# The second row of each q and k block starts later, and the copy of its transposes is queued two half chunks behind them

## The chip, the cores and the metric

The kernel runs on one core of one Trainium2 chip. The metric is the device time of one launch in microseconds (us). The core has a matrix engine (PE, with its weight loads PEld), a vector engine (DVE), a scalar engine (ACT), a general engine (POOL) and an engine that issues most transfers (SP). Each works through its own queue in the order in which the program issued its instructions, and waits on the others by semaphores.

## The reference

One layer of a hybrid block for 256 positions of width 2048, in float32:

```python
xn = rms_norm(x, norm1_g)
q, k, v, ga, gg = split(xn @ w_in)              # q, k: 4 heads x 2 x 128; v: 4 heads x 256
q = apply_rope(rms_norm(q, q_norm_g), cos, sin)
k = apply_rope(rms_norm(k, k_norm_g), cos, sin)
att = rms_norm(diff_attention(q, k, v, lam), subln_g) * (1 - lambda_init)
u = silu(layer_norm(causal_depthwise_conv(ga * sigmoid(gg), conv_w, conv_b)))
h = x + concat([att, u]) @ w_out
y = h + (silu(rms_norm(h) @ w_gate) * (rms_norm(h) @ w_up)) @ w_down
```

`diff_attention` makes two softmax maps for each head and subtracts lam times the second from the first. The mask lets a query see the 64-wide chunks up to its own.

## The kernel before

**Chunks.** All weights stream through the core in chunks. In the first part of the kernel a chunk is 256 rows of one 512-column block (two k-tiles of 128 rows). Each chunk n is loaded (SP, line 315), rounded to a high part by ACT (line 320, here called whi(n)), and the rest is taken by DVE (line 329, here wlo(n)). PE then multiplies in two halves: half A is eight matmuls with the high weights (lines 359 and 360), half B is four matmuls with the low weights (line 365). There are three buffers each for high and low parts, so whi(n) can run only when half A of chunk n-3 is through. Rounding and splitting are issued two chunks ahead (`run_chunks`, lines 387 to 419).

**Chunk numbers.** The blocks follow one another: chunks 0 to 32 are the convolution's columns, 33 to 40 k block 0, 41 to 48 q block 0, 49 to 56 k block 1, 57 to 64 q block 1, 65 to 72 v block 0, 73 to 80 v block 1. Then comes w_out: 81 and 82, 83 and 84, 85 and 86 are its first three column blocks with rows 0 to 511 (attention heads 0 and 1), 87 to 92 the same column blocks with rows 512 to 1023 (heads 2 and 3, head 3 first in chunk 88), 93 to 104 the convolution's rows, 105 to 112 the last column block. Gate, up and down projections follow until the end.

**Steps between the chunks.** All other work is written as generators. `resume()` (line 244) is called after each half chunk and advances every running generator to its next `yield`; `lag(n)` (line 250) lets n half chunks pass. What a generator issues lands in the engines' queues at that place. Convolution taps (DVE, line 517) are put in by `run_side` as long as a credit lasts (1.30 us more per half chunk; each wlo, tap and listed step spends some).

**The q and k rows.** When a block is summed, `qk_done` (line 590) starts one `qk_rows` generator (line 606) per 128 positions (m = 0 and 1, the two rows). A row issues: 4 squares on ACT (lines 612 and 427), three small operations on POOL for the scale fq (lines 217, 218, 615); 3 half chunks later 4 scaled copies qn on ACT (line 619); 2 later the rotation on DVE (lines 626 to 629); 6 later, as soon as an auxiliary bank is free (`room`, line 257: of the 4 auxiliary PSUM banks `held[0]` are counted as taken), 4 transposes on PE (line 634) and, right behind them, the copy to qT or kT on ACT (line 635), after which the row counts as placed. The second row starts two half chunks behind the first.

**Who waits for the rows.** After a q block `qk_done` waits until all four rows of q and k are placed, and starts `attend_scores` for two heads, 4 half chunks apart (lines 595 to 602). A head's steps, each some half chunks after the one before: scores on PE (line 649), maximum on DVE (657, 659), exponentials on ACT (668), reciprocal on DVE (677) and a small product a on POOL (679), p on ACT (688), the difference wt on DVE (695), 3 transposes on PE (701 to 703) and their copy on ACT (706). `v_done` (709) copies v out of its sum banks on ACT (712) and starts `attend_values` (718): once the head's 706 is issued, products with v on PE (727), squares (427) on ACT, their scale ro on POOL (217, 218), att on ACT (738), 4 transposes on PE (746) and the split into high part (233, ACT) and low part (234, DVE) for w_out.

**Sum banks.** There are 4 for the chunks, two per block in turn, so that chunk 83 takes the two of v block 1.

**Where w_out waits for a head.** `operand()` (line 332) asks for the split attention output; if the step that makes it has not been issued, it issues all taps that are left and calls `resume()` until it is there, with no matmuls between.

Of the kernel before, what the change touches and what calls it, by code (L numbers as in the profile page):

```python
# [64 lines left out]
AUX = 4  # L65

LAG = (3, 2, 6)
HL_BUFS = 3

KTILE_US = 1.30  # L70
# [52 lines left out]
def tile_block(  # L123
# [82 lines left out]
    def negative_lambda():  # L206

        le = const.tile([P, 2], F32, tag="le", name="le")
        act.activation(le, ls, AF.Exp)
        pool.tensor_tensor(neg_lam, le[:, 1:2], le[:, 0:1], ALU.subtract)  # L210
        pool.tensor_scalar(neg_lam, neg_lam, 1.0, -LAMBDA_INIT, ALU.mult, ALU.add)

    def rsqrt_mean(dst, ss, n, eps):

        k = dst.shape[-1]
        t = small.tile([P, 8], F32, tag="rsq", name="rsq")
        pool.tensor_scalar(t[:, :k], ss, 1.0 / n, eps, ALU.mult, ALU.add)
        pool.tensor_tensor(dst, t[:, :k], neghalf[:, :k], ALU.pow)
# [22 lines left out]
    def start(gen):  # L241
        running.append(gen)
# [7 lines left out]
    def lag(n):  # L250
        for _ in range(n):
            yield


    held = [0]

    def room(n, hold=0):
        while held[0] + n > AUX:
            yield
        held[0] += hold  # L260
# [6 lines left out]
    def spend(us):  # L267
        credit[0] -= us
# [49 lines left out]
    def round_chunk(c):  # L318
        c["hi"] = c["view"](wp.tile([P, NK * N], F32R, tag="whi", name="whi", bufs=HL_BUFS))
        act.copy(c["hi"], c["raw"])  # L320
        if c["by_dma"]:
            c["lo"] = c["view"](wp.tile([P, NK * N], F32R, tag="wlo", name="wlo", bufs=HL_BUFS))
            act.activation(c["lo"], c["raw"], AF.Copy, scale=-1.0)
            pool.dma_start(out=c["lo"], in_=c["raw"].bitcast(F32R), accum_op=ALU.add)

    def split_chunk(c):
        if not c["by_dma"]:
            c["lo"] = c["view"](wp.tile([P, NK * N], F32R, tag="wlo", name="wlo", bufs=HL_BUFS))
            dve.tensor_tensor(c["lo"], c["raw"], c["hi"].bitcast(F32), ALU.subtract)  # L329
# [95 lines left out]
    def square_sum(src, accum, **kw):  # L425
        junk = pre.tile([P, N], F32, tag="junk", name="junk", bufs=1)
        act.activation(junk[:, : src.shape[-1]], src, AF.Square, accum_out=accum, **kw)
# [162 lines left out]
    def qk_done(key, b, ps):  # L590
        for m in range(NM):
            yield
            start(qk_rows(key, b, m, ps[m]))
            yield
        if key == "q":
            while not all((k, b, m) in placed for k in "qk" for m in range(NM)):
                yield
            if b == 0:
                negative_lambda()
            for hd in (2 * b, 2 * b + 1):  # L600
                start(attend_scores(hd))
                yield from lag(4)
# [3 lines left out]
    def qk_rows(key, b, m, ps):  # L606

        G = N // DH
        spend(1.65)
        ss = small.tile([P, G], F32, tag="ssq", name="ssq")  # L610
        for j in range(G):
            square_sum(ps[:, j * DH : (j + 1) * DH], ss[:, j : j + 1], scale=rstd1[m])
        f = small.tile([P, G], F32, tag="fq", name="fq")
        rsqrt_mean(f, ss, DH, EPS)
        pool.tensor_scalar(f, f, rstd1[m], 0.0, ALU.mult, ALU.add)
        yield from lag(LAG[0])
        qn = pre.tile([P, G, DH], F32, tag="va", name="qn")
        for j in range(G):
            act.activation(qn[:, j, :], ps[:, j * DH : (j + 1) * DH], AF.Copy, scale=f[:, j : j + 1])
        yield from lag(LAG[1])  # L620
        t1 = pre.tile([P, G, DH], F32, tag="vb", name="t1")
        t2 = pre.tile([P, G, DH], F32, tag="vc", name="t2")
        tab = gcs[key, m]
        hd = DH // 2
        bc = lambda ap, n: ap.unsqueeze(1).to_broadcast([P, G, n])
        dve.tensor_tensor(t1, qn, bc(tab[:, 0, :], DH), ALU.mult)
        dve.tensor_tensor(t2[:, :, :hd], qn[:, :, hd:], bc(tab[:, 1, :hd], hd), ALU.mult)
        dve.tensor_tensor(t2[:, :, hd:], qn[:, :, :hd], bc(tab[:, 1, hd:], hd), ALU.mult)
        dve.tensor_tensor(t1, t1, t2, ALU.add)
        yield from lag(LAG[2])  # L630
        yield from room(1)
        pt = aux_ps.tile([P, G, P], F32, tag="aux", name="ps_qk")
        for j in range(G):
            pe.transpose(pt[:, j, :], t1[:, j, :], ident)
        act.copy(qkT[key][:, b * G : (b + 1) * G, m * P : (m + 1) * P], pt)
        placed.add((key, b, m))

# [536 lines left out]
    for b in range(2):  # L1174
        done += [lambda ps, key=key, b=b: qk_done(key, b, ps) for key in "kq"]
# [71 lines left out]
```

## Time and profile before

| | |
|---|---|
| median of 3 runs | 1048.78 us (1048.51 to 1048.9) |
| the profiled execution's own time | 1048.92 us |
| its span | 1047.1 us |
| PE busy | 1036.2 us, 99% of the span |
| DVE, ACT, POOL busy | 900.6, 621.6, 100.5 us |
| granted PE clock | 1.00 in every stretch |

The span is what the profile covers; 1.8 us of the execution's own time lie around it. In the rows of a timeline stand the start in us from the span's start, the duration in us, the engine, the line, the operation with output and inputs, and in brackets how long the engine was idle before it and who released it. Matmuls overlap, so the start of one to the start of the next is what a matmul costs, not its duration. Chunk n's half B (line 365, x4) is the mark by which a chunk can be found: chunk 54 has it at 157.86 us, chunk 56 at 164.74, chunk 72 at 215.39, chunk 77 at 235.84, chunk 82 at 249.94, chunk 88 at 272.65.

### The profile page before, as it was taken

The page shows a single profiled execution, that of the slowest core. Times are in us where ns is not written, and L with a number is a line of the kernel's source. Part 1 is how long each engine was busy: PE and PEld are TensorE (multiplying, and loading weights), DVE is VectorE, ACT ScalarE, POOL GpSimd, SP SyncE. Part 2 cuts the span into 40 slices and gives each one's busy share as a digit, 9 for nine tenths or more (in the row PEclk, how much of TensorE's full clock was granted, in tenths as well). Part 3 has the DMA queues.
Part 4 walks back from the last instruction along what each step waited for, and adds up shares of the span by engine and source line. Part 5 has one row for each costly group of instructions (what it writes and reads, how often), then busy time and mean ns, then how long its engine had stood idle before and what let it go on. Part 6 is the DMA issues. An engine that isn't in the chain of part 4 may idle for free.

```text
span 1047.1 us, 12933 instructions
## 1 busy us (share of the span) xinstructions
PE 1036.2 (99%) x4663; PEld 852.5 (81%) x4663; DVE 900.6 (86%) x1095; ACT 621.6 (59%) x786; POOL 100.5 (10%) x143
## 2 busy tenths in 40 slices
PE   9999999999999999999999999999999999999998
PEld 7888887877788788888888888888888888888886
DVE  7899889898765599999787898999878789989897
ACT  7544666755756565776463657666644446657442
POOL 0130122201100100000001010000000110000010
PEclk9999999999999999999999999999999999999999
DMA  9657654453546566987867789879757879798683
GB/s 335 227 182 280 212 163 167 154 181 134 177 153 226 194 223 214 268 266 236 232 210 188 217 271 273 256 217 285 248 175 241 219 208 291 222 287 267 187 265 85
DMA packets 113936, 231.30 MB, mean 221 GB/s; under 512 B 7504, under 2 KB 8656, under 8 KB 113616
## 3 DMA queue, kind: packets, MB, share of 16 engines
q1 hardware_dynamic: 104864, 203.71, 56.9%
q0 software_dynamic: 8864, 26.74, 13.4%
q8 instruction: 36, 0.59, 0.2%
q14 instruction: 28, 0.23, 0.1%
q10 hardware_dynamic: 144, 0.03, 0.0%
HBM read 204.24 MB, written 9.44 MB: 204 GB/s over the span
## 4 chain that ended last, share of the span: by engine, by line
PE 61%; DMA 2%; DVE 2%; issue 1%; ACT 0%; DVEq 0%; POOLq 0%
PE q L1020 12%; PE q L1014 12%; PE q L1015 12%; PE q L995 8%; PE q L993 7%; PE q L994 7%; DMA raw<-in_w_down_dram 1%; PE ps_a L831 1%; DMA wlo<-raw 1%; PE acc L365 1%; PE acc L359 1%; PE acc L360 1%; DVE wlo L329 1%; DVE wlt L976 0%; DVE wt L966 0%
## 5 line engine op out<-in xcount | busy, mean ns | idle before, releaser
L320 ACT CAST whi<-raw 128x1024 fp32r<-128x1024 f32 (+1 forms) x273 | 281.5, 1048 | 141.6 <-PE acc L360 58.9
L329 DVE TENSOR_TENSOR wlo<-raw,whi 128x1024 fp32r<-128x1024 f32 (+1 forms) x239 | 287.8, 1218 | 73.5 <-ACT whi L320 73.3
L972 ACT CAST wh<-wt 128x2048 fp32r<-128x2048 f32 x52 | 99.6, 1914 | 77.6 <-DVE wt L968 76.9
L976 DVE TENSOR_TENSOR wlt<-wt,wh 128x2048 fp32r<-128x2048 f32 x52 | 119.1, 2290 | 14.9 <-ACT wh L972 14.7
L359 PE MATMUL acc<-whi,xhi 128*128 128x512 f32 x320 | 126.9, 397 | 1.0 <-ACT whi L320 0.9
L360 PE MATMUL acc<-whi,xlo 128*128 128x512 f32 x320 | 125.2, 391 | 0.0
L1014 PE MATMUL q<-whi,chi 128*128 128x512 f32 x320 | 125.2, 391 | 0.0
L1015 PE MATMUL q<-whi,clo 128*128 128x512 f32 x320 | 124.5, 389 | 0.0
L993 PE MATMUL q<-wh,fhi 128*128 128x512 f32 x280 | 109.9, 393 | 0.0
L994 PE MATMUL q<-wh,flo 128*128 128x512 f32 x280 | 109.1, 390 | 0.0
L517 DVE SCALAR_TENSOR_TENSOR y<-upad,cw,y 128x256 f32<-128x256 f32 x240 | 102.2, 482 | 2.2 <-ACT y L510 2.2
L1014 PE MATMUL q<-whi,ahi 128*128 128x512 f32 x256 | 100.2, 391 | 0.0
L1015 PE MATMUL q<-whi,alo 128*128 128x512 f32 x256 | 99.6, 389 | 0.0
L975 DVE TENSOR_TENSOR wlb<-wb,wh 128x1536 fp32r<-128x1536 f32 x52 | 91.1, 1752 | 1.8 <-ACT wh L969 1.8
L365 PE MATMUL acc<-wlo,xhi 128*128 128x512 f32 x320 | 87.8, 396 | 2.0 <-DVE wlo L329 2.0
L1020 PE MATMUL q<-wlo,chi 128*128 128x512 f32 x320 | 85.7, 390 | 0.2 <-DMA wlo<-raw 0.2
L969 ACT CAST wh<-wb 128x1536 fp32r<-128x1536 f32 x52 | 76.6, 1474 | 0.0
L365 PEld LDWEIGHTS acc<-wlo,xhi 128*128 128x128 f32 x320 | 59.7, 189 | 15.3 <-DVE wlo L329 3.3
L359 PEld LDWEIGHTS acc<-whi,xhi 128*128 128x128 f32 x320 | 60.4, 189 | 14.3 <-ACT whi L320 1.9
L1020 PEld LDWEIGHTS q<-wlo,chi 128*128 128x128 f32 x320 | 59.9, 188 | 13.2 <-DMA wlo<-raw 0.8
L360 PEld LDWEIGHTS acc<-whi,xlo 128*128 128x128 f32 x320 | 60.4, 189 | 12.2
L1014 PEld LDWEIGHTS q<-whi,chi 128*128 128x128 f32 x320 | 60.1, 188 | 12.3
(230 smaller groups left out, 1739.1 us busy)
## 6 DMA issues: line engine op xcount, KB each, us to landing
raw<-in_w_in_dram SPq DMA_DIRECT2D x79, 512.0 KB, 4.6
raw<-in_w_down_dram SPq DMA_DIRECT2D x64, 512.0 KB, 7.2
raw<-in_w_gate_dram SPq DMA_DIRECT2D x48, 512.0 KB, 7.5
raw<-in_w_up_dram SPq DMA_DIRECT2D x48, 512.0 KB, 6.2
wb<-in_w_up_dram SPq DMA_DIRECT2D x40, 512.0 KB, 3.7
wb<-in_w_gate_dram SPq DMA_DIRECT2D x40, 512.0 KB, 4.9
wlo<-raw POOLq DMA_DIRECT2D x34, 512.0 KB, 7.1
raw<-in_w_out_dram SPq DMA_DIRECT2D x32, 512.0 KB, 4.2
```

What stands on the lines that cost most here:

```text
L320: act.copy(c["hi"], c["raw"])
L329: dve.tensor_tensor(c["lo"], c["raw"], c["hi"].bitcast(F32), ALU.subtract)
L359: pe.matmul(ps[m], xhi[:, ms], hi[:, j, :], start=c["first"] and j == 0, stop=False)
L360: pe.matmul(ps[m], xlo[:, ms], hi[:, j, :], start=False, stop=False)
L365: pe.matmul(ps[m], xhi[:, ms], lo[:, j, :], start=False, stop=c["last"] and j == nk - 1)
L517: dve.scalar_tensor_tensor(y[:, ct, :], src, wk, y[:, ct, :], ALU.mult, ALU.add)
L976: dve.tensor_tensor(lot, c["t"], c["hi"][:, :SUMMED].bitcast(F32), ALU.subtract)
L993: pe.matmul(ps, hi, c["hi"][:, w], start=bool(first), stop=False)
L994: pe.matmul(ps, lo, c["hi"][:, w], start=False, stop=False)
L1014: pe.matmul(ps, xs[i][0][:, ms], hi[:, i, :], start=i == 0 and bool(c["first"].get(qs[m])), stop=False)
L1015: pe.matmul(ps, xs[i][1][:, ms], hi[:, i, :], start=False, stop=False)
L1020: pe.matmul(sum_bank(c, qs[m]), xs[i][0][:, ms], lo[:, i, :], start=False, stop=i == 1 and bool(c["last"].get(qs[m])))
```

## The change

`qk_done` lets four half chunks pass, where it was one, between the start of a row and the next turn of its loop, so the second row starts five half chunks behind the first instead of two. In `qk_rows` the auxiliary bank of the transposes is counted as held until the copy is issued, and the copy (and with it the mark that the row is placed) is issued two half chunks behind the transposes. Nothing is computed differently, and no instruction is added or taken away.

```diff
+ROWS_APART, COPY_LAG = 4, 2
@@ qk_done
         for m in range(NM):
             yield
             start(qk_rows(key, b, m, ps[m]))
-            yield
+            yield from lag(ROWS_APART)
@@ qk_rows
         yield from lag(LAG[2])
-        yield from room(1)
+        yield from room(1, 1)
         pt = aux_ps.tile([P, G, P], F32, tag="aux", name="ps_qk")
         for j in range(G):
             pe.transpose(pt[:, j, :], t1[:, j, :], ident)
+        yield from lag(COPY_LAG)
+        held[0] -= 1
         act.copy(qkT[key][:, b * G : (b + 1) * G, m * P : (m + 1) * P], pt)
         placed.add((key, b, m))
```

## The prediction

> **What bounds the kernel now.** I read the page's busy times first, then who PE waited for in the stretch that the change touches (120 to 300 us), then the stretches, then the timelines of PE, DVE, ACT and POOL there.
>
> ```profile
> PE 1036.2 (99%) x4663; PEld 852.5 (81%) x4663; DVE 900.6 (86%) x1095; ACT 621.6 (59%) x786; POOL 100.5 (10%) x143
> PE acc L365 <- DVE wlo L329: 2.0, 2, 1.2
> PE acc L359 <- DVE mchi L582: 0.6, 1, 0.6
> PE ps_o L727 <- ACT qT L706: 0.6, 1, 0.6
> PE ps_o L727 <- ACT v L712: 0.3, 1, 0.3
> 60.00:120.00 60.00, 60.00 (x273) 49.66 (x272) 59.62 (x109) 29.02 (x35) 1.53 (x3) 1.00 0.66 231
> ```
>
> PE is the bound: 99% busy, so a microsecond in which PE stands still is a microsecond of the kernel, and what other engines gain is worth nothing by itself. In the touched stretch PE stood still for 2.0 + 0.6 + 0.6 + 0.3 = 3.5 us. That is the ceiling of any gain. DVE is full in the convolution part (59.62 of 60 us), so it has little room to catch up. PE's issue order loses or gains no instruction.
>
> ```profile
> 148.50 3.40 POOL L218 TENSOR_TENSOR fq<-rsq,neghalf 128x4 f32<-128x4 f32 x1
> 152.31 1.14 ACT L619 ACTIVATE qn<-acc,fq 128x128 f32<-128x128 f32 x4 [1.61 <-POOL fq L615]
> 154.42 1.23 DVE L329 TENSOR_TENSOR wlo<-raw,whi 128x1024 fp32r<-128x1024 f32 x1 [3.39 <-ACT whi L320]
> 155.56 0.68 DVE L626 TENSOR_TENSOR t<-qn,gcsq 128x512 f32<-128x512 f32 x1
> 157.56 1.27 DVE L517 SCALAR_TENSOR_TENSOR y<-upad,cw,y 128x256 f32<-128x256 f32 x3
> 158.75 1.22 DVE L329 TENSOR_TENSOR wlo<-raw,whi 128x1024 fp32r<-128x1024 f32 x1
> 159.89 0.68 DVE L626 TENSOR_TENSOR t<-qn,gcsq 128x512 f32<-128x512 f32 x1
> 155.14 1.07 PE L365 MATMUL acc<-wlo,xhi 128*128 128x512 f32 x4
> 157.86 1.07 PE L365 MATMUL acc<-wlo,xhi 128*128 128x512 f32 x4
> 164.74 1.20 PE L365 MATMUL acc<-wlo,xhi 128*128 128x512 f32 x4 [0.80 <-DVE wlo L329]
> 215.39 1.20 PE L365 MATMUL acc<-wlo,xhi 128*128 128x512 f32 x4 [1.24 <-DVE wlo L329]
> ```
>
> This shows how the two larger waits come about. A chunk is 2.72 us of PE (157.86 - 155.14). A row's rotation is 2.0 us of DVE (155.56 to 157.56), a tap 0.4, a wlo 1.14 (158.75 to 159.89). ACT stood for fq, whi(54) came late, DVE stood 3.39 us, and then got two rotations in two successive chunks: 2.0 + 3 x 0.4 + 1.14 = 4.3 us for chunk 55, with a fourth tap 4.7 for chunk 56. Against 2.72 it falls back 1.6 and then 2.0 us; its lead at chunk 54 was 157.86 - 155.65 = 2.2. So PE waited 0.80 at chunk 56, and 1.24 by the same pattern at chunk 72.
>
> **The change part by part.** Nothing is added; steps move.
>
> *The rotations five half chunks apart.* In the new order the DVE work before each wlo, from chunk 55, is: one rotation, 3 taps, 3 taps, rotation with 4 taps. With wlo that is 3.1, 2.3, 2.3, 4.7 us, or +0.4, -0.4, -0.4, +2.0 against PE. The furthest DVE falls back is 1.6, inside its lead of 2.2: the wait of 0.80 goes. The same holds for 1.24 at chunk 72. The wait of 0.3 for v goes too, since its product moves two chunks on. **Gain 2.0 + 0.3 = 2.3.** The bounds are 0 (waits stay) and 2.3.
>
> *The copy two half chunks later.* Its bank is held meanwhile. Counted through the code, no step is refused a bank for it. With the second row 3 half chunks later, the block's last copy is 5 later, so all four heads start 5 half chunks later. The blocks that do not depend on them (v, w_out) stay. The rest of the sum is what is late then.
>
> *Chunks 68 to 74.* ACT's new queue there is: p, four exponentials, whi(68), squares, whi(69), copy, p, qn, whi(70), copy, squares, whi(71). By the rows below an exponential group is 1.6 us, p 0.8, a whi 0.95; the squares are about as long as the exponentials, qn 1.0. That makes about 13 us in the time of four chunks, 10.9 plus about 1.2 of inserted PE work. ACT falls back about 1 us from a lead of up to 2, and fq can cost it as much again. **Loss between 0 and 1.7; I take 0.5**, nearer to the load, which rows show, than to the waits.
>
> ```profile
> 235.84 1.18 PE L365 MATMUL acc<-wlo,xhi 128*128 128x512 f32 x4
> 241.48 0.36 ACT L668 ACTIVATE pr<-ps_s,nmx 128x128 f32<-128x128 f32 x1
> 243.08 1.05 ACT L320 CAST whi<-raw 128x1024 fp32r<-128x1024 f32 x1
> 239.61 0.17 DVE L657 MEMSET ps_s<- 64x128 f32 x1
> 241.06 1.27 DVE L517 SCALAR_TENSOR_TENSOR y<-upad,cw,y 128x256 f32<-128x256 f32 x3
> 248.69 0.22 DVE L677 RECIPROCAL r<-sm 128x2 f32<-128x2 f32 x2
> 249.38 0.90 ACT L688 ACTIVATE p<-pr,a 128x128 f32<-128x128 f32 x2 [3.99 <-POOL a L679]
> 250.19 0.46 ACT L706 COPY qT<-ps_wt 128x384 f32<-128x384 f32 x1
> 246.85 1.07 PE L365 MATMUL acc<-wlo,mahi 128*128 128x512 f32 x4
> 249.94 1.07 PE L365 MATMUL acc<-wlo,mahi 128*128 128x512 f32 x4
> 254.54 1.08 PE L365 MATMUL acc<-wlo,mahi 128*128 128x512 f32 x4
> 193.27 1.95 POOL L679 TENSOR_TENSOR a<-r,neg_lam 128x1 f32<-128x1 f32 x2 [6.87 <-DVE r L677]
> ```
>
> *Chunk 83 waits for v.* Count from E, the half B of chunk 77 (235.84), behind head 1's transposes: DVE needs these, so its lead is set anew there. In before, head 3's reciprocal stands 12.85 later; ACT waits 0.69 for a, p takes 0.81. Now head 2's reciprocal stands at this place, behind 1.4 us more DVE work (a maximum of 1.45 for a wt of 0.66, two taps, less a reciprocal). Behind its p ACT has head 3's exponentials (1.60, 241.48 to 243.08) and only then v, whose first half takes 0.64. That is 12.85 + 1.4 + 0.69 + 0.81 + 1.60 + 0.64 = E + 18.0, and 0.3 to 0.9 more by how much later DVE reaches E. Chunk 83 takes the banks of v block 1, so its first matmul waits for this copy. It began at 254.54 - 8 x 0.227 = E + 16.9 in before. Now the 0.37 of a head's transposes at chunk 81 (3.09 against 2.72) and the 1.88 of the product at chunk 82 (4.60 against 2.72) come later, and head 3's scores (1.36) come before: E + 16.0. **Loss 2.0 to 2.9; I take 2.4.**
>
> *Chunk 84 waits for head 2's copy.* Then ACT has whi(84), whi(85), head 3's p, whi(86), and behind them this copy (706), for which PE stands behind half A of chunk 84. DVE: wlo(84) at E + 21.2, wt, reciprocal at 22.0; a between 0.7 and 1.95; p, whi(86), copy: E + 24.9 to 26.2. PE would start the product at E + 24.0 (18.4 + 2.72 + 1.81 + the 1.06 from transposes to product that the pattern takes in before). **Loss 1.0 to 2.3; I take 1.6.** Both ends of these two losses reach down to 0 if DVE should be a chunk further ahead.
>
> ```profile
> 257.27 0.27 PE L701 MATMUL ps_wt<-ident,wt 128*128 128x128 f32 x1
> 258.33 1.56 PE L727 MATMUL ps_o<-v,qT 128*128 128x256 f32 x6 [0.57 <-ACT qT L706]
> 261.29 0.47 ACT L233 ACTIVATE ahi<-ps_at,cols 128x256 fp32r<-128x256 f32 x1 [2.27 <-PE ps_at L746]
> 261.80 0.48 DVE L234 SCALAR_TENSOR_TENSOR alo<-ps_at,cols,ahi 128x256 fp32r<-128x256 f32 x1 [2.09 <-ACT ahi L233]
> 262.32 0.47 ACT L233 ACTIVATE ahi<-ps_at,cols 128x256 fp32r<-128x256 f32 x1 [0.55 <-DVE alo L234]
> 262.69 0.38 ACT L427 ACTIVATE junk<-ps_o 128x256 f32<-128x256 f32 x1
> 263.56 1.04 ACT L320 CAST whi<-raw 128x1024 fp32r<-128x1024 f32 x1
> 265.08 0.84 ACT L738 ACTIVATE att<-ps_o,ro 128x256 f32<-128x256 f32 x2 [0.48 <-POOL ro L218]
> 255.20 1.95 POOL L218 TENSOR_TENSOR ro<-rsq,neghalf 128x2 f32<-128x2 f32 x1
> ```
>
> *Chunk 88 waits for head 3.* Its split was issued 3 half chunks before chunk 88 and comes 4 later. So `operand` issues it by one resume ahead of chunk 88's first matmul, with nothing between. Count from X, the end of half A of chunk 86. PE: transposes of head 3 (0.33), of head 2 (0.44), product (start X + 1.0, 1.2), half B and chunk 87: X + 5.9; unhindered, chunk 88's second matmul would start at about X + 6.5. ACT: copy, the two halves of head 2's split 1.03 apart, squares (0.87) done at X + 3.3; ro 1.5 to 2.6; att 0.74; whi(90) 0.95; the first high part 0.5. DVE: wlo(90), then the low part: X + 8.2 to 9.3, which that matmul needs. **Loss 1.7 to 2.8; I take 2.2.** With ACT and DVE free it would still be about 1.0, the high and low part one behind the other.
>
> **Sum:** -2.3 + 0.5 + 2.4 + 1.6 + 2.2 = +4.4 on the profiled execution's 1048.92, which lies 0.14 above the median: 1053.3, or **1053.2** against the median.
>
> [...]
>
> **The rivals.**
> - *Nothing is gained.* The squares that covered fq's 3.40 us now come behind qn, so ACT may wait as long and DVE stand its 3.39 still; if both waits stay, 1055.2. Against it: the rotations are no longer in successive chunks.
> - *Not slower.* DVE's lead at chunk 77 decides. If head 2's reciprocal comes 3 us earlier from E than I reckon, v and the copy are in time, and chunk 88 costs 1.5: -2.3 + 1.5, 1048.0. For it: DVE's 3.39 of idle time may be filled. Against it: E is set by PE, and 12.85 of the 14.25 us is DVE work of before.
> - *The clock.* A wait of PE longer than any here (the largest is 1.24) might bring down the granted clock, 1.00 so far; a chunk at half the clock is 2.72 more, 1055.9 or above. [...]
> - *Faster* would take chunk 88 at 0 as well, which nothing shows.
>
> **How the numbers follow.** Forecast 0.60 (by its own bounds 1051 to 1056.5), nothing gained 0.12, clock 0.06, not slower 0.17, faster 0.05. Range 1049.8 to 1057: it leaves out most of the last two and little above. A measurement of this kernel tells about 0.2% (2.1 us) from no change: slower 0.78, same 0.17, faster 0.05.
>
> **What would show it.** In the changed profile: no PE wait for wlo at chunks 56 and 72; a wait of line 359 for v (712) of 2 us or more at chunk 83; a longer wait of line 727 for line 706 at chunk 84; a wait of lines 359 and 360 for the split (233, 234) of head 3 at chunk 88. If DVE's reciprocal of head 2 lies less than 12 us behind E, the two middle terms are wrong; if lines 359 and 360 don't wait at chunk 88, the fourth is.

## The result, and the profile after

The changed kernel takes **1051.78 us** (median of 14 runs, 1051.25 to 1057.92) against 1048.77 for the kernel before beside it (14 runs, 1048.0 to 1050.59): 1.0031 times as long, 95% interval 1.0023 to 1.0039. The profiled execution took 1051.79 us (span 1050.0), 2.87 more than the profiled one of before. Lines 68 and on of before are one higher in the new kernel, those from 635 on three higher.

The page's busy times, and PE's waits between 120 and 300 us (who waits, for whom; us in total, times, longest):

```profile
PE 1036.6 (99%) x4663; PEld 853.5 (81%) x4663; DVE 901.1 (86%) x1095; ACT 624.1 (59%) x786; POOL 101.7 (10%) x143
```
```profile
PE acc L360 <- ACT v L715: 2.1, 1, 2.1
PE acc L361 <- DVE alo L235: 0.8, 1, 0.8
PE acc L360 <- DVE mchi L583: 0.6, 1, 0.6
PE acc L360 <- ACT ahi L234: 0.6, 1, 0.6
PE ps_o L730 <- ACT qT L709: 0.6, 1, 0.6
```

Busy times tell little: PE's is 0.4 us longer. The waits tell more. The two for wlo are gone, as is the 0.3 for v at a product. In their place stand 2.1 us for v, and 0.6 and 0.8 for a split (lines 234 and 235). Idle time went from 3.5 to 4.7 us, 1.2 of the 2.9 that the kernel is slower; PE's timeline and the granted clock (the column ahead of the DMA share) show more:

```profile
246.94 1.07 PE L366 MATMUL acc<-wlo,mahi 128*128 128x512 f32 x4
250.14 0.50 PE L360 MATMUL acc<-whi,mahi 128*128 128x512 f32 x1 [2.13 <-ACT v L715]
...
251.21 0.63 PE L361 MATMUL acc<-whi,malo 128*128 128x512 f32 x1
...
253.34 1.52 PE L366 MATMUL acc<-wlo,mahi 128*128 128x512 f32 x4
254.70 0.39 PE L360 MATMUL acc<-whi,mahi 128*128 128x512 f32 x1
257.58 1.56 PE L730 MATMUL ps_o<-v,qT 128*128 128x256 f32 x6 [0.57 <-ACT qT L709]
271.84 0.50 PE L360 MATMUL acc<-whi,ahi 128*128 128x512 f32 x1 [0.62 <-ACT ahi L234]
273.12 0.50 PE L361 MATMUL acc<-whi,alo 128*128 128x512 f32 x1 [0.78 <-DVE alo L235]
```
```profile
250.00:251.00 1.00, 0.86 (x3) 0.58 (x4) 0.02 (x1) 1.00 (x3) 0.00 (x0) 0.93 0.82 252
251.00:252.00 1.00, 1.00 (x3) 0.78 (x3) 0.37 (x1) 1.00 (x2) 0.00 (x0) 0.50 0.96 272
252.00:253.00 1.00, 1.00 (x4) 0.74 (x3) 1.00 (x2) 0.55 (x1) 0.00 (x0) 0.50 1.04 403
253.00:254.00 1.00, 1.00 (x4) 0.81 (x3) 1.00 (x6) 0.00 (x0) 0.33 (x1) 0.50 0.37 127
254.00:255.00 1.00, 1.00 (x5) 0.77 (x5) 1.00 (x3) 0.41 (x1) 1.00 (x2) 0.86 0.83 256
```

Behind the wait of 2.13 us a matmul lasts 0.63 us instead of 0.39 (start to start 0.43 instead of 0.227), until about 254: the granted clock was 0.50. That is loss too, and no view of waits or busy time has it (PE counts as busy). From the column: 0.07 + 3 x 0.50 + 0.14 = 1.71 us.

To place gain and loss, take the start of each chunk's half B in both traces and subtract. The differences against before, set to 0 at chunk 55 (the profiled executions start up to 0.4 us apart; by chunk 98 nothing changes any more), for this kernel and some of those below. The chunk columns come from one execution of each kernel, the profiled one, whose own time stands beside the median; in filled and v_early it was the slowest:

| kernel | median us | profiled us | chunk 81 | 83 | 84 | 87 | 88 | 98 |
|---|---|---|---|---|---|---|---|---|
| after | 1051.78 | 1051.79 | -2.99 | -1.56 | -1.11 | +0.21 | +2.73 | +2.76 |
| filled | 1052.33 | 1054.73 | -2.99 | -2.71 | -1.20 | +1.69 | +5.47 | +5.89 |
| v_early | 1054.29 | 1055.18 | -2.99 | -5.24 | -1.18 | +1.91 | +5.58 | +6.09 |
| v_early_filled | 1049.99 | 1050.61 | -2.99 | -5.24 | -2.33 | -1.05 | +1.49 | +1.51 |
| head3_early | 1052.5 | 1052.23 | -2.99 | -1.83 | -1.10 | +1.36 | +1.62 | +3.73 |
| p_late | 1047.69 | 1047.26 | -2.99 | -5.24 | -5.21 | -3.76 | -1.28 | -1.28 |
| p_late3 | 1050.19 | 1050.3 | -2.99 | -5.24 | -5.21 | -2.63 | -2.37 | +1.32 |

(In chunks 82 to 87 lie attention products and transposes whose place moved, so that the columns 83 to 87 compare only kernels with the same places.) The change gains 3.0 us up to chunk 81 and loses 5.7 from 82 to 88.

How the two waits of chunks 83 and 84 come about stands in ACT's timeline, with POOL's and DVE's:

```profile
246.30 0.23 DVE L680 RECIPROCAL r<-sm 128x2 f32<-128x2 f32 x2
246.99 0.91 ACT L691 ACTIVATE p<-pr,a 128x128 f32<-128x128 f32 x2 [4.24 <-POOL a L682]
249.39 1.28 ACT L715 ACTIVATE v<-acc,rstd 128x512 f32<-128x512 f32 x2
250.53 2.01 ACT L321 CAST whi<-raw 128x1024 fp32r<-128x1024 f32 x2
254.12 0.41 ACT L691 ACTIVATE p<-pr,a 128x128 f32<-128x128 f32 x1 [1.57 <-POOL a L682]
255.65 0.51 ACT L691 ACTIVATE p<-pr,a 128x256 f32<-128x256 f32 x1 [1.13 <-POOL a L682]
256.07 1.04 ACT L321 CAST whi<-raw 128x1024 fp32r<-128x1024 f32 x1
257.05 0.48 ACT L709 COPY qT<-ps_wt 128x384 f32<-128x384 f32 x1
```

First head 2's p and four exponentials of head 3 (247.8 to 249.4) stand ahead of v, then head 3's p stands ahead of the copy out of head 2's transposes, and itself waits 1.57 and 1.13 us for a.

### The profile page after: what moved, and what is told of

It is laid out like the page before. It is cut to its first block, busy times and chain, and to the rows that moved or that the text cites. A ratio compares the mean times of both kernels' runs of the same rounds, so it can differ in the third digit from the quotient of the medians.

```text
span 1050.0 us, 12935 instructions
## 1 busy us (share of the span) xinstructions
PE 1036.6 (99%) x4663; PEld 853.5 (81%) x4663; DVE 901.1 (86%) x1095; ACT 624.1 (59%) x786; POOL 101.7 (10%) x143
## 4 chain that ended last, share of the span: by engine, by line
PE 62%; DVE 1%; DMA 1%; issue 0%; ACT 0%; DVEq 0%
PE q L1017 12%; PE q L1023 12%; PE q L1018 12%; PE q L998 8%; PE q L996 8%; PE q L997 8%; PE acc L366 1%; DMA wlo<-raw 1%; PE ps_a L834 1%; PE acc L360 1%; PE acc L361 1%; DVE wlo L330 0%; DVE wlt L979 0%; DVE wt L969 0%; ACT wh L975 0%
## 5 line engine op out<-in xcount | busy, mean ns | idle before, releaser
L321 ACT CAST whi<-raw 128x1024 fp32r<-128x1024 f32 (+1 forms) x273 | 282.0, 1049 | 153.9 <-PE acc L361 67.7
L1018 PEld LDWEIGHTS q<-whi,clo 128*128 128x128 f32 x320 | 60.1, 188 | 12.3
```

Of the source, the lines that this page charges most:

```text
L1018: pe.matmul(ps, xs[i][1][:, ms], hi[:, i, :], start=False, stop=False)
```

## The experiments

My theory after this: gain and loss are two things. The rows' distance takes the waits for wlo away; what comes back is a queue on ACT, in which what PE needs next (v, then head 2's copy) stands behind steps that nobody needs yet, and the half clock behind the long wait adds to it (1.71 us behind 2.13). The rival: the gain is PE's lead over ACT and DVE, which comes back at the heads whatever their order.

**filled.** PE is kept busy in the wait for v.

```diff
+        if c is chunks[83]:
+            warm_up(18)        # transposes of the identity into a bank of their own
```

> The changed kernel with 18 transposes of the identity (into a spare bank, results unused) put on PE between chunk 82 and chunk 83, where PE stood 2.13 us for v and then ran at half the clock for about 3 us. Theory (the clock's loss takes the place of the wait for head 2's copy at chunk 84): no gap at chunk 83, clock 1.00 all through, but PE now waits some 1.8 us more than 0.57 for that copy behind half A of chunk 84, and the time stays within 0.6 of the changed kernel's 1051.8. Rival (the clock's loss of 1.7 us comes on top of everything): no new wait at chunk 84, 1050.1.

1052.33 us (1.0031, 1.0020 to 1.0043). PE's waits, and the granted clock:

```profile
PE ps_o L732 <- ACT qT L711: 2.1, 1, 2.1
```
```profile
259.00:262.00 3.00, 3.00 (x9) 2.32 (x8) 1.99 (x4) 2.58 (x7) 0.89 (x2) 0.50 0.76 255
276.00:279.00 3.00, 3.00 (x12) 2.59 (x11) 0.00 (x0) 0.72 (x2) 0.00 (x0) 0.50 0.58 220
```

The clock stays up at chunk 83 (1.00 up to 258 us), but PE comes to chunk 84 earlier, waits 2.1 us there for head 2's copy, and the half clock follows that wait. As theory had it, the second wait stood behind the first; what it had not is another stretch of half clock, behind the 0.64 and 0.78 us of chunk 88. That is the profiled execution, the slowest of six (1054.73; the fastest took 1051.04).

**v_early.** v's second block is copied (line 715) right behind chunk 80, ahead of head 3's exponentials, where `v_done` runs one half chunk later.

```diff
-    def v_done(b, ps):
-        yield
+    def v_copy(b, ps):
         for m in range(NM):
             act.activation(v_sb[m][:, b * N : (b + 1) * N], ps[m], AF.Copy, scale=rstd1[m])
+    def v_start(b, ps):        # called when the block is summed
+        if b:
+            v_copy(b, ps)
+        return v_done(b, ps)
+    def v_done(b, ps):
+        yield
+        if not b:
+            v_copy(b, ps)
```

> The changed kernel with the copies of v block 1 issued right behind chunk 80, ahead of head 2's p and head 3's exponentials in ACT's queue. Theory (chunk 83 stands for v because ACT does head 3's exponentials first): the wait at chunk 83 and the half clock go (4.1 us), and the wait for head 2's copy behind half A of chunk 84 grows by 1.9 to 3.3 since PE is there earlier; about 1050.4, between 1049.7 and 1051.2. Rival (what the change costs does not sit there): 1051.8.

1054.29 us (1.0040, 1.0027 to 1.0054): slower, a miss for both. PE's and ACT's timeline, and the clock:

```profile
255.95 2.93 PE L739 MATMUL ps_o<-v,qT 128*128 128x256 f32 x6 [3.43 <-ACT qT L709]
252.55 0.40 ACT L691 ACTIVATE p<-pr,a 128x128 f32<-128x128 f32 x1 [1.57 <-POOL a L682]
...
255.43 0.47 ACT L709 COPY qT<-ps_wt 128x384 f32<-128x384 f32 x1
```
```profile
256.00:262.00 6.00, 6.00 (x14) 4.81 (x15) 3.75 (x7) 2.73 (x7) 0.89 (x2) 0.50 0.50 175
```

The wait for v is gone and all of it stands again at chunk 84, where the wait grew by 2.9 us (0.57 to 3.43), as theory had it. What theory had not is the clock: twice the half clock follows, 0.35 + 3.00 + 0.06 = 3.4 us by the column of 255 to 263, and 1.7 more at chunk 88 (275 to 280).

**head3_early.** Head 3's transposes two half chunks sooner, so that its split is there for chunk 88.

```diff
-        yield from lag(4)
+        yield from lag(2 if hd == 3 else 4)
```

> The changed kernel with head 3's transposes of its weights issued two half chunks earlier (2 instead of 4 behind wt), so that its split is issued in the middle of chunk 87 and nothing has to be issued ahead of chunk 88's first matmul. Theory (chunk 88's two waits cost about 2.0 with their restarts): they go but for some 0.3, 1050.0. Rival (they are covered by something else that is late then): 1051.8.

1052.5 us (1.0039, 1.0026 to 1.0051): a miss. **both_early** has this edit and v_early's.

> The changed kernel with both edits, v block 1 copied right behind chunk 80 and head 3's transposes two half chunks earlier. Theory (the two losses are separate and add): the sum of the two gains, 1048.6, about where the kernel before was, with a wait of 2 to 3 us left behind half A of chunk 84. Rival (one loss takes the place of the other): no better than the better of the two alone, about 1050.

1054.38 us (1.0048, 1.0035 to 1.0060): a miss as well. PE's timeline of head3_early:

```profile
249.60 0.50 PE L360 MATMUL acc<-whi,mahi 128*128 128x512 f32 x1 [2.11 <-ACT v L715]
272.29 0.50 PE L361 MATMUL acc<-whi,alo 128*128 128x512 f32 x1 [0.54 <-DVE alo L235]
289.13 0.49 PE L360 MATMUL acc<-whi,mchi 128*128 128x512 f32 x1 [1.69 <-DVE mchi L583]
```

At chunk 88 the wait fell from 1.40 to 0.54 us, and the table's row shows it (+1.62 for +2.73). At chunk 93 it came back: 1.69 for 0.63. The normalised convolution (mchi) is issued when the taps run out; in the kernel after, `operand` issues the last taps early because head 3's split isn't there at chunk 88, and without that the convolution's transposes move from half A to half B of chunk 88 in the order. The profiled execution of both_early (1052.22) shows the same 1.69 and, at chunk 84, 3.45 us for the copy.

**p_late.** v early, and head 3's p three half chunks later, behind head 2's copy; head 3's transposes keep their place.

```diff
-        yield from lag(2)
+        yield from lag(5 if hd == 3 else 2)
         p1s = []
...
-        yield from lag(4)
+        yield from lag(1 if hd == 3 else 4)
         yield from room(1)
```

> This is the kernel after with v's second block copied behind chunk 80 and, besides, ScalarE's scalings (p) of head 3 moved three half chunks later, behind the copy of head 2's transposes; the three half chunks are taken out again ahead of head 3's own transposes. With v early alone the copy out of head 2's transposes came at 255.43 us, behind head 3's p, which waited 1.57 and 1.13 us for GpSimd; TensorE stood 3.43 us for it. Theory (the copy's place in ScalarE's order, behind head 3's p, sets the wait at chunk 84): that wait falls from 3.4 to under 1 us and takes the clock's half speed behind it away; the time falls from 1054.3 to 1049-1050.5, of which up to 1 us may come back where head 3's split is later. Rival (the copy is late because of its own chain, its transposes or head 2's wt): the wait stays above 2.5 us and the time at about 1054.

**1047.69 us** (11 runs, 1047.26 to 1048.46) against 1048.71 for the kernel before beside it (23 runs): 0.9989, 0.9980 to 0.9998. It is faster than both kernels, if by 0.1% only, and 1.3 us better than theory had it, which did not count the half clock at chunk 88. PE's waits, and ACT's timeline:

```profile
PE acc L361 <- DVE alo L235: 0.8, 1, 0.8
PE acc L360 <- DVE mchi L583: 0.6, 1, 0.6
PE acc L360 <- ACT ahi L234: 0.6, 1, 0.6
PE ps_o L739 <- ACT qT L709: 0.6, 1, 0.6
```
```profile
249.03 2.96 ACT L321 CAST whi<-raw 128x1024 fp32r<-128x1024 f32 x3
252.60 0.48 ACT L709 COPY qT<-ps_wt 128x384 f32<-128x384 f32 x1 [0.61 <-PE ps_wt L706]
```

The copy runs at 252.60 instead of 255.43 and now waits for PE's transposes. The wait of 3.4 us is 0.57, the clock 1.00 throughout. So the place in ACT's queue was the cause, not the copy's own chain. The rival that PE's lead comes back whatever the order falls too, as far as chunk 87: the lead there is 3.76 us, where the kernel after is 0.21 behind.

**p_late_alone.** The edit of p_late without v early.

> The kernel after with head 3's p three half chunks later, but v's second block copied where the kernel after copies it, behind head 3's exponentials. Theory (two waits of ScalarE's order stand one behind the other, for v at chunk 83 and for head 2's copy at chunk 84, and either holds the time by itself): the v wait of 2.1 us at chunk 83 stays, with the half clock behind it, and the time is that of the kernel after, 1051.0-1052.3 us. Rival (the place of p alone was what cost): 1047.5-1049 us.

1051.65 us (1.0027, 1.0018 to 1.0037), with the same 2.1 us for v and the same half clock (0.50 from 251 to 254) as the kernel after. Either of the two waits holds the time alone; both have to go.

**v_early_filled.** The clock's price by itself.

```diff
         o = aux_ps.tile([P, NM, E], F32, tag="aux", name="ps_o")
+        if hd == 2:
+            for _ in range(27):
+                pe.transpose(o[:, 0, :P], ident, ident)
```

> V early alone (1054.3 us), with 27 transposes of the identity put ahead of head 2's products, into their own bank, which the products overwrite: TensorE is busy for about 3.2 of the 3.4 us in which it stood for head 2's copy. Theory (the wait costs its 3.4 us, and the clock at 0.50 behind it another 3 to 4 us over chunks 84 and 88): no row under 0.9 of the clock, and 1050.6 us (1050.0-1051.5), which is the 1047.7 us of the kernel without that wait and 2.9 us more. Rival (the clock at half speed costs little, because what waits behind it waits for ScalarE anyway): 1053.5-1054.5 us.

1049.99 us (1.0015, 1.0006 to 1.0023), at the lower end of what theory had. The same products wait for the same copy (they start at 256.12, in v_early at 255.95, which is the same place counted from chunk 55), but PE does idle work meanwhile, and the clock holds:

```profile
255.00:262.00 7.00, 6.50 (x32) 5.33 (x31) 6.12 (x12) 4.75 (x10) 0.89 (x2) 1.00 0.46 150
272.00:279.00 7.00, 7.00 (x36) 5.71 (x35) 3.32 (x5) 3.76 (x6) 0.00 (x0) 1.00 0.40 153
```

Of v_early's median of 1054.29, 4.3 us are the clock's, and 2.3 (1049.99 less p_late's 1047.69) the wait's. The five executions of v_early lie between 1052.1 and 1055.18, so the clock's part is no fixed number.

**rows_only** (`ROWS_APART, COPY_LAG = 4, 0`) and **copy_only** (`1, 2`, the rows' distance of before) are the two halves of the change.

> The four half chunks between the rows alone, the copy out of the bank straight behind the transposes again (no two half chunks). The heads start three half chunks later than before instead of five. Theory (the two wlo waits go with the rows' distance alone, worth 3.0 us; what comes back is set by how head 2's transposes, its copy and its products stand in one half chunk): no wait for v, but a wait of 2.5-3.5 us for head 2's copy at chunk 83 with some 2 us of half clock behind it, and 1052.5-1055 us. Rival (what comes back goes with the number of half chunks that the heads are later, 5.7 us for five): 3.4 us come back for three, and 1049.5 us.

> The rows one half chunk apart as in the kernel before, and only the copy out of the bank two half chunks behind the transposes; the heads start two half chunks later. Theory (the two wlo waits of 0.80 and 1.24 us go with the distance of the rows): both stay, so that nothing is gained, and the later heads cost 0.5-4 us: 1049.3-1052.8 us. Rival (the copy's lag takes the waits away): both gone, 1046-1048 us.

1055.46 us (1.0063, 1.0051 to 1.0075) and 1058.09 us (1.0092, 1.0078 to 1.0106): each half alone is slower than both together, and both times lie above what theory had. PE's timelines, of rows_only and of copy_only:

```profile
220.08 1.20 PE L366 MATMUL acc<-wlo,xhi 128*128 128x512 f32 x4 [0.16 <-DVE wlo L330]
239.04 1.76 PE L652 MATMUL ps_s<-kT,qT 128*128 128x256 f32 x4 [3.65 <-DVE malo L235]
```
```profile
194.68 0.50 PE L360 MATMUL acc<-whi,xhi 128*128 128x512 f32 x1 [1.94 <-ACT whi L321]
217.03 1.21 PE L366 MATMUL acc<-wlo,xhi 128*128 128x512 f32 x4 [1.12 <-DVE wlo L330]
240.83 2.05 PE L652 MATMUL ps_s<-kT,qT 128*128 128x256 f32 x4 [3.02 <-DVE malo L235]
```

With the rows' distance alone the two wlo waits are gone (one of 0.16 us stands at chunk 74). With the copy's lag alone the wait of chunk 72 stays, 1.12, so there the gain is the distance's, as theory had it. That of chunk 56 goes with either half, which theory had not. DVE's wlo(54), in the kernel after and in copy_only, shows what differs from before:

```profile
153.49 1.23 DVE L330 TENSOR_TENSOR wlo<-raw,whi 128x1024 fp32r<-128x1024 f32 x1 [2.20 <-ACT whi L321]
```
```profile
152.30 1.23 DVE L330 TENSOR_TENSOR wlo<-raw,whi 128x1024 fp32r<-128x1024 f32 x1 [2.28 <-ACT whi L321]
```

DVE stood 2.2 and 2.3 us here, where it stood 3.39 in the kernel before, so its lead over PE at chunk 54 was 3.5 us instead of 2.2 (2.6 in rows_only). In copy_only that lead carries it through two rotations in successive chunks without a wait of PE. At chunk 56 the distance is therefore not shown to be what counts; why DVE's stand is shorter is left open.

But in rows_only the wait of 3.65 us stands at a place that no theory named: head 3's scores (ps_s, chunk 77) want the auxiliary bank that head 1's split is still reading, and DVE has head 2's maximum, four taps and a wlo ahead of that split. In the whole change the heads are two half chunks later and the scores stand one chunk further on, clear of it. So the copy's lag does something for this change, and none of these traces shows that it is by the bank that it holds.

**rows_lag4** and **rows3_lag4** try to keep the gain with the heads near their old places: `ROWS_APART, COPY_LAG = 4, 0` and `3, 0`, and for both `LAG = (3, 2, 4)` for `(3, 2, 6)`.

> Rows four half chunks apart, no wait ahead of the copy, a lag of 4 for 6: the heads start one half chunk later than before. By the theory of a separate gain and loss: 3.0 us gained, and 0.9-2.5 us lost at chunk 82, where only one half chunk is left between head 2's transposes and its products; 1046.5-1048.5 us. Rival (the lead is given back): 1049-1051 us.

> Rows three half chunks apart instead of four, no wait ahead of the copy, and the transposes two half chunks sooner (a lag of 4 for 6): every head starts at the half chunk at which it starts in the kernel before. Theory (gain and loss are two things: the gain comes from the rows' distance, the loss from the heads' later start): both wlo waits are gone, 3.0 us gained, the waits of the heads are those of before but for up to 1 us because TensorE arrives earlier; 1046.5 us (1045.8-1047.5). Rival (TensorE's lead is given back at the heads whatever their start, since ScalarE and VectorE do not come along): waits of 2 us and more at chunks 82 to 88, 1048.5-1050 us.

1056.9 us (1.0081, 1.0069 to 1.0093) and 1051.34 us (1.0022, 1.0013 to 1.0030). Both miss. PE's timelines, of rows_lag4 and of rows3_lag4:

```profile
232.70 1.55 PE L652 MATMUL ps_s<-kT,qT 128*128 128x128 f32 x8 [2.20 <-DVE malo L235]
255.91 2.93 PE L730 MATMUL ps_o<-v,qT 128*128 128x256 f32 x6 [3.64 <-ACT qT L709]
```
```profile
192.64 0.50 PE L360 MATMUL acc<-whi,xhi 128*128 128x512 f32 x1 [1.80 <-ACT whi L321]
218.21 0.63 PE L635 MATMUL ps_qk<-ident,t 128*128 128x128 f32 x4 [0.72 <-DVE t L630]
253.32 1.56 PE L730 MATMUL ps_o<-v,qT 128*128 128x256 f32 x6 [0.42 <-ACT v L715]
```

In rows3_lag4, with the heads where they were, chunks 82 to 88 wait as in before (0.42 and 0.57). That does not show that the loss there comes from the heads' later start: PE comes to chunk 81 some 2.0 us later than in before (counted from chunk 41), so it has no lead to give back. The gain is not kept. In ACT's order squares and exponentials now meet ahead of whi(63); directly ahead of whi(65), for which PE waits 1.80 us at chunk 65, stand a p, a copy and four exponentials, and the p itself waits for POOL, whose product a takes 3.22 us there:

```profile
189.05 0.51 ACT L691 ACTIVATE p<-pr,a 128x256 f32<-128x256 f32 x1 [2.41 <-POOL a L682]
```

The transposes, two half chunks sooner, wait for the rotations. So gain and loss were not had apart here: in each of these shifts a generator came to stand beside another somewhere.

**p_late3.** p_late, with head 3's later steps two half chunks sooner.

```diff
-        yield from lag(5 if hd == 3 else 2)
+        yield from lag(4 if hd == 3 else 2)
...
-        yield from lag(2)
+        yield from lag(1 if hd == 3 else 2)
```

> The kernel with v early and head 3's p behind head 2's copy (1047.7 us), with the later steps of head 3 two half chunks sooner (p two half chunks later instead of three, wt one half chunk behind p): head 3's output transposes stand at chunk 87 and no longer directly ahead of the chunk 88 that needs their split. Theory (the 0.59 and 0.78 us of waits at chunk 88 come from that place, and cost some 2.0 us with their restarts): both go, a second wait of 0.57 us for head 3's copy comes (0.9 us with its restart), and the time is 1046.6 us (1046.0-1047.3), under both kernels. Rival (head 3's wt or its split is late by VectorE whatever the place): waits of 1.4 us and more stay, 1047.5-1049 us.

1050.19 us (1.0008, 0.9999 to 1.0016): a miss. The 0.59 us wait of chunk 88 goes and the other falls from 0.78 to 0.54, but as in head3_early the convolution comes half a chunk later, and PE waits at chunk 93; the timeline, and the clock:

```profile
285.32 0.50 PE L360 MATMUL acc<-whi,mchi 128*128 128x512 f32 x1 [1.69 <-DVE mchi L583]
```
```profile
286.00:289.00 3.00, 3.00 (x8) 2.25 (x8) 1.59 (x2) 0.33 (x1) 0.00 (x0) 0.50 0.38 137
```

## Why the prediction was right, and where it was not

The forecast was 1053.2 us, slower; measured are 1051.78, slower. Step by step, on the profiled executions (+4.4 forecast, +2.87 found, of which 0.36 is the start):

- *Gain, 2.3.* Both wlo waits went. The reason given, the rows' distance, is shown for chunk 72 (copy_only keeps that wait); at chunk 56 DVE's lead was also 1.3 us longer than the working took it, and copy_only shows that this alone is enough. DVE's new order of work (one rotation, 3 taps, 3 taps, a rotation with 4 taps) came as worked out. The size lies outside the bound of 2.3: 2.99 us by chunk 81, without the 0.3 for v, which lies at chunk 82 and went too. Each of these two waits cost more than its idle time. Ahead of it PE's last matmul counts 0.39 us where it takes 0.227 (0.16), behind it the four of half B take 1.20 where they take 1.07 otherwise (0.13): 0.29 for each wait. That makes 0.80 + 1.24 + 2 x 0.29 = 2.62; for 0.37 I have no row.
- *Chunks 68 to 74, 0.5.* Nothing was lost: between 120 and 248 us PE waits for nobody, and counted as in the table chunk 63 stands at -1.09 and chunk 71 at -1.19. ACT's lead held.
- *Chunk 83, 2.4.* 2.13 of idle time, 2.4 with its ends. The working held: head 2's reciprocal lies 246.30 - 231.88 = 14.42 behind chunk 77's mark (forecast 14.25, and 0.3 to 0.9 more), PE was ready 15.97 behind it (forecast 16.0).
- *The clock, a rival at 0.06.* It came true beside the forecast, not instead of it. I took 1.24 us, the longest wait of before, for the edge of what is known, put the price at a chunk at half clock (2.72) and the chance at next to nothing, though my own sum held a wait of 2.4 us. It cost 1.71.
- *Chunk 84, 1.6.* Right in the copy's time: it ends at 257.05 + 0.48 = 257.53, which is 25.65 behind the mark (forecast 24.9 to 26.2). Wrong in the loss: the wait is the 0.57 of before, because PE came 1.71 us later through the half clock. The two terms are one. filled shows it: with the clock up, 2.07 us of wait are there, and chunk 84 stands at -1.20 in filled, at -1.11 in the kernel after. In the kernel after the slow stretch ends ahead of this wait, and the wait is 1.5 us shorter (0.57 against 2.07).
- *Chunk 88, 2.2.* 0.62 + 0.78, with their ends 1.98. The step was issued out of `operand`, the high and low parts one behind the other, as worked out: the low part is ready 8.6 us behind the end of chunk 86's half A (forecast 8.2 to 9.3).

With the sizes measured: -2.62 - 0.37 - 0.4 (v, with its ends) + 2.4 + 1.71 + 1.98 = +2.7, against 2.87 - 0.36 = 2.5. Against that the forecast of +4.4 was 1.9 high: 1.1 in the gain, 0.5 in chunks 68 to 74, 0.1 in the three losses together (6.2 forecast, 6.1 found), and 0.2 without a row.

The rival *nothing is gained* falls (the wlo waits are gone). *Not slower* falls by the number that was to decide it: DVE's reciprocal came 0.1 to 0.7 us earlier than reckoned, not 3. Of the two a, head 3's took POOL 1.95 us, the long end of the working's 0.7 to 1.95, and head 2's 0.81. Not settled: whether any order of these steps keeps the whole gain. p_late keeps 1.28 of 2.99, and its remaining loss at chunk 88 (2.5 us in the table, of which 2.0 are the waits) was removed in p_late3 only at the price of chunk 93.

## What to carry to other kernels

When a step is moved in an in-order queue, list what it now stands ahead of, and who needs that next: here 3 us won by one reordering were lost because v and a copy, which PE needed at once, stood behind exponentials and scalings that could wait. Removing the first of two waits in a row (2.13 us, in v_early) lengthened the second here from 0.57 to 3.43 us, so find the second before judging the first. And charge a long wait of the matrix engine with the clock stretch that may follow it, or fill it: here nine of twelve waits of 1.80 to 3.65 us had a granted clock of 0.50 behind them, and idle transposes in the wait took 4.3 us off v_early.

## What the runs showed of the hardware

A wait of PE of 1.80 to 3.65 us was followed by a granted clock of 0.50 in nine of twelve cases in the profiled executions; the three without are 3.45 us (both_early), 2.20 (rows_lag4) and 1.80 (rows3_lag4). Of the waits of 1.69 us (chunk 93) one in five had it, and two of the six pairs of 0.6 and 0.8 us at chunk 88 (filled and v_early, not after, p_late, p_late_alone and v_early_filled). The length of a wait alone does not decide. The length of the slow stretch is steadier: the loss by the clock column is 1.71 us in the kernel after and in filled (0.11 + 1.50 + 0.10), 3.4 in v_early, 1.7 for each of the two of copy_only (0.49 + 1.00 + 0.21 for the first), that is 3.4 us at half speed, or twice that.

A 1 us row at 0.89 has 0.22 us of half clock in it, and with each start worked out like this, the two stretches of filled start at 258.78 and 275.84, 17.06 us apart, those of v_early 20.48 and those of copy_only 44.36, which is 5, 6 and 13 times 3.41. In the kernel after, the clock falls once more behind the last matmul (0.79 in the row of 1049 to 1050), by the same working at 1049.58, 234 times 3.413 us behind the start at 250.86. Ahead of a stretch stood waits of 1.69 us (p_late3), of 1.94 (copy_only), and twice two waits that make some 1.4 us together (0.64 and 0.78 in filled, 1.40 by the idle time of 272 to 275 in v_early).

From these starts an estimate: laid out in steps of 3.41 us, in each trace from its own start, the idle time within one step sorts the cases better than the length of a wait. In the nine traces with a stretch between 60 and 310 us, all nine steps with 1.94 us or more of PE waits between 120 and 300 us are followed by half clock, and between 1.40 and 1.69 three of five are. Of those with 1.28 us or less one is, the 0.65 us in the first half of v_early's long stretch. The 2.20 us of rows_lag4, with no half clock behind it, falls across an edge, 1.07 and 1.13 us; for the 3.45 us of both_early and the 1.80 of rows3_lag4, traces without such a start, no run shows it. A sharp threshold these runs do not give: 1.69 us in copy_only had no half clock behind it, 1.40 in v_early had. What sets the step is not shown.

Executions of one kernel differ too: the 11 of p_late3 fall into four of 1047.78 to 1048.94 us, with mean clocks of 1.0 or 0.999, and seven of 1049.57 to 1050.66, all at 0.998.
